# Row maxima of layer 1 started 32 product steps later with their loads placed behind the weight pieces, and the third row tile's input read into a second buffer

## The chip, the cores and the metric

The kernel runs on one core of one Trainium2 chip. A core has five instruction streams that run beside each other: TensorE (PE, with its weight loads shown as PEld), VectorE (DVE), ScalarE (ACT), GpSimd (POOL) and SyncE (SP). SP does no arithmetic; it issues most of the DMA transfers, one after the other, and a transfer whose buffer is not free yet holds up those behind it. ACT and POOL issue some transfers as well. The metric is the time of one execution on the device in microseconds; a kernel's time is the median of its runs.

## What is computed

Two layers over 2048 latent tokens of width 1024 and 256 context tokens. The change lies in layer 1, which is 2-D neighbourhood attention with 16 heads of width 64:

```python
h = rms_norm(x, norm_g[i]) * (1 + scale) + shift
q, k, v, z = jnp.split(jnp.dot(h, w_in), 4, axis=-1)
...
s_lat = jnp.einsum('bqhd,brkhd->bhqrk', qr, kb) * scale + bias
s_lat = jnp.where(col_mask, s_lat, -jnp.inf)
s_ctx = jnp.einsum('bqhd,bchd->bhqc', qr, k_ctx) * scale
p = jax.nn.softmax(jnp.concatenate([s_lat, s_ctx], axis=-1), axis=-1)
...
y = jnp.dot(o * jax.nn.silu(z_x), w_out)
```

The token grid has 32 rows of 64 columns; each query sees a window of 8 x 16 latent keys and all context keys. The softmax subtracts the maximum of each query's row of scores. The kernel computes these maxima ahead of the attention, in a pass of their own.

## The kernel before

The 2304 tokens (context first) are 18 row tiles of 128, numbered 0 to 17; tiles 0 and 1 are context. Float32 operands are split into a high and a low part, and a product takes three matmuls for each of the 8 pieces of the inner dimension (`mm3_steps`, L131 to L133). One such triple is a product step; a cell (t, j), row tile t by 512 columns j, has 8 steps.

Every instruction is issued by one engine in a fixed order. That order is not the program's text alone: when the kernel is built, a scheduler with its own estimates of durations orders each engine's instructions, taking among those that it holds to be ready the one that stands first in the text. `issue_after(x)` binds it: what is traced inside the block comes behind x on x's engine. On the chip the order stays as it is, whether the estimates were right or not.

Three stages follow each other around the change.

**`odd_qk`, the query/key stage.** Cells run over the row tiles with j = 2, 3 (keys), 0, 1 (queries) and 4 (first half of the values). Each tile's input is made ready by `prep`: `transposed` (L338) loads 128 x 1024 values of x1 into a buffer x (L346, on SP), ScalarE squares them into a PSUM bank, POOL makes the reciprocal root, VectorE scales, TensorE transposes; `modulate` scales and shifts on ScalarE, VectorE writes the parts hhi and hlo (two buffers each), and ScalarE's queue stores the result to H (L382) for the next stage. The buffer x exists once, so the next tile's load waits for that store. Tiles 0 and 1 are prepared at the end of the stage before, tile 2 after the cells of tile 0, and so on. Behind a cell of products, ScalarE squares its result (osq), VectorE sums it (oss), POOL takes the root (L218, L220), VectorE scales (onat, L1545), TensorE transposes (L1554) and ScalarE evicts (oqh). The pool osA, on the left side of the memory, is opened here; its buffer hx, of the size of x, is used for the last row tile alone.

**`odd_vz`, the value/gate stage.** It starts with tiles 15, 16 and 17 and then goes down to 0; j = 5 (second half of the values), 6 and 7 (gates, with VectorE's product L1639, transposes L1642 and ScalarE's ozt), and 4 for tiles 0 to 14. The 65 cells are 520 product steps; the first cells are (15,5), (16,5), (15,6), (16,6), (15,7), (16,7). The weights of a column block are 8 pieces of 256 KB (`od_steps`, `split_steps`): each is loaded into one of three buffers wraw (L422, on SP; `self.wload` is the last such load that was traced) and split by ScalarE (w3h for j = 7) and VectorE (w3l, L426), both bound behind the eviction of the cell in which the piece is traced. `turn(3)` traces three pieces a cell; the last three of j = 7 are traced in the stage's third cell.

Woven into the products are the row maxima, `maxes`: for each of 16 heads the keys mk (L1670, one load for two heads) and a bias table mtab (L1672) are loaded, POOL adds the row and the column mask to the table (L1673, L1674), and 16 steps follow. Every fourth step loads a strip of queries mq (L1682), which ScalarE writes into mz; each step has a matmul against the context keys (L1688), one against a rectangle of latent keys (L1695), and VectorE reduces both to maxima (L1690, and L1701 with the table). They share five PSUM banks mx. `row` transposes a head's maxima and stores them to M1.

`weave(main, side, ratio, lag, head)` traces both: after each step of main it adds ratio to due, which starts at -head x ratio, and traces one step of side for each whole unit. It binds each step of main behind the side step lag + 1 back. Here the ratio is 0.57 and the lag 15; the 256 side steps are the maxima.

**`odd_attention`.** Its loads go through `load` (L113), which binds each behind the one before, so SP issues them as one chain: the query parts of head 1, first keys, values, the two bias tables, context keys, the query parts of head 0, further keys, the context values V1c and the mask maskk. The memory of this stage lies over that of odd_vz; POOL then adds the mask to the tables (L1782). The first scores are against the context (kc, L1785 and L1786); scores against the latent keys (kt) get their bias on VectorE (L1944), which needs the masked tables.

Of the kernel before, what the change touches and what calls it, by code (L numbers as in the profile page):

```python
# [10 lines left out]
F32 = mybir.dt.float32  # L11
F32R = mybir.dt.float32r
# [5 lines left out]
P = 128  # L18
D = 1024
# [3 lines left out]
T = SEQ + CTX  # L23
# [38 lines left out]
def rect(kind, g, c):  # L62

    (r, nr), (k, nk) = reach(kind, 0, g), reach(kind, 1, c)
    while nr * nk < 256:
        k, nk = (k, nk + 1) if k == 0 else (k - 1, nk + 1)
    return (r, nr), (k, nk)


def even(a, n):  # L70

    b = a // 2 * 2
    return b, (a + n + 1) // 2 * 2 - b, a - b


def pieces(kind, ax, g, a, n):

    blocks, u = BLOCKS[kind][ax], AXES[ax][2]
    out = []
    for p in range(n):  # L80
        i = blocks.index((g, a + p) if (g, a + p) in blocks else (1, a + p - u * (g - 1)))
        if out and out[-1][1] + out[-1][2] == i:
            out[-1][2] += 1
        else:
            out.append([p, i, 1])
    return out


class Kern:
# [240 lines left out]
        self.prp = self.pool(es, name, bufs=2, side=side, reuse_waits="tile")  # L330
        self.hbufs, self.wbufs = bufs, wbufs

    def prep(self, l, t, src, pp, tag, last=None):

        parts = None if l else self.parts()
        return self.modulate(l, t, *self.transposed(t, src, pp, tag, None, parts), last)

    def parts(self):  # L338
        return [self.tl(self.prp, [P, KD, P], "h" + z, F32R, bufs=self.hbufs) for z in ("hi", "lo")]
# [1 line left out]
    def transposed(self, t, src, pp, tag, xp, parts):  # L341

        nc, sp = self.nc, self.prp
        pool, tg = xp or (sp, "x")
        x = self.tl(pool, [P, D], tg, bufs=1 if tg == "x" else None)
        self.xload = nc.sync.dma_start(x[:], src[t * P : t * P + P, :])  # L346
        ss = self.tl(sp, [P, 2], "ssx")
        ps = [self.tl(pp, [P, 4, P], tag[0], bufs=tag[1]) for _ in range(2)]
        if parts:
            self.act(parts[1][:].rearrange("p k t -> p (k t)"), x[:], AF.Square, accum_out=ss[:, 0:1])  # L350
            self.rpow(ss[:, 1:2], ss[:, 0:1], 1.0 / D, EPS)
            nc.vector.tensor_scalar(out=x[:], in0=x[:], scalar1=ss[:, 1:2], scalar2=None, op0=ALU.mult)
        else:
            for g in range(2):
                self.act(ps[g][:].rearrange("p k t -> p (k t)"), x[:, self.HALF[g]], AF.Square, accum_out=ss[:, g : g + 1])
            nc.gpsimd.tensor_scalar(out=ss[:, 1:2], in0=ss[:, 0:1], scalar1=ss[:, 1:2], scalar2=EPS * D, op0=ALU.add, op1=ALU.add)
            nc.gpsimd.tensor_tensor(out=ss[:, 1:2], in0=ss[:, 1:2], in1=self.mhalf[:, :1], op=ALU.pow)
            nc.vector.tensor_scalar(out=x[:], in0=x[:], scalar1=ss[:, 1:2], scalar2=D ** 0.5, op0=ALU.mult, op1=ALU.mult)
        for k in range(KD):
            nc.tensor.transpose(ps[k // 4][:, k % 4, :], x[:, k * P : k * P + P], self.ident[:])  # L360
        return x, ps, parts
# [1142 lines left out]
    def odd_qk(self, ws, win, hT):  # L1504
        nc = self.nc
# [5 lines left out]
        with ExitStack() as es:  # L1511
            sp = self.pool(es, "osA", bufs=2, side="left", reuse_waits="tile")
            pp = self.pool(es, "opA", bufs=2, space=PSUM, reuse_waits="tile")
# [2 lines left out]
            nc.vector.tensor_scalar(out=qkg[:, 0:1], in0=qkg[:, 0:1], scalar1=0.125, scalar2=None, op0=ALU.mult)  # L1516
            self.later += [self.od_steps(win, j, ws, lambda: self.done) for j in (0, 1)]
            pend, kt = [], {}
            prep = lambda t, last=None: self.prep(1, t, self.x1, pp, ("px", 2), last)

            def cell(t, j):
                if (t, j) == (NT - 3, 3):
# [90 lines left out]
    def odd_vz(self, ws, win, hT):  # L1613
        nc = self.nc
        self.z1 = self.scr("z1", (KD, P, SEQ), F32)
        self.M1 = self.scr("M1", (16, SEQ), F32)
        NR, NC = (len(b) for b in BLOCKS["q"])
        with ExitStack() as es:
            sp = self.pool(es, "osB", bufs=2, side="left", reuse_waits="tile")
            mp = self.pool(es, "omB", bufs=2, side="left", reuse_waits="tile")  # L1620
            pp = self.pool(es, "opB", bufs=2, space=PSUM, reuse_waits="tile")
            mk = self.tl(mp, [P, NR + NC], "maskq", bufs=1)
# [33 lines left out]
            def row(h, mc):  # L1656
                pt = self.tl(pp, [P, 512], "mx", bufs=5)
                nc.tensor.transpose(pt[:16, :P], mc[:], self.ident[:])
                r = self.tl(mp, [P, P], "mr", F32R, bufs=1)
                self.act(r[:16], pt[:16, :P], AF.Copy, scale=-1.0)  # L1660
                for g in range(4):
                    nc.gpsimd.dma_start(self.M1[h, g * 512 : g * 512 + 512].rearrange("(a c b) -> c a b", a=8, c=4),
                                        r[4 * g : 4 * g + 4].rearrange("c (a b) -> c a b", a=8).bitcast(F32))

            def maxes():
                for h in range(16):
                    j, b = h // 2, (h % 2) * 64
                    if b == 0:
                        k = self.tl(mp, [P, T], "mk", F32R, bufs=2)
                        nc.sync.dma_start(k[:].bitcast(F32), self.K1[j])  # L1670
                    tb = self.tl(mp, [P, NR, NC], "mtab", bufs=2)
                    nc.sync.dma_start(tb[:], self.i["rpb_q"][h].rearrange("p (r c) -> p r c", r=NR))  # L1672
                    nc.gpsimd.tensor_tensor(out=tb[:], in0=tb[:], in1=mk[:, :NR].unsqueeze(2).to_broadcast([P, NR, NC]), op=ALU.add)  # L1673
                    nc.gpsimd.tensor_tensor(out=tb[:], in0=tb[:], in1=mk[:, NR:].unsqueeze(1).to_broadcast([P, NR, NC]), op=ALU.add)  # L1674
                    m = self.tl(mp, [P, 16, 5], "mm")
                    nc.vector.memset(m[:], -3e38)
                    kl = k[:, CTX:].rearrange("d (r c) -> d r c", r=32)
                    for R in range(16):
                        g, c = divmod(R, 4)
                        if c == 0:  # L1680
                            q = self.tl(mp, [P, 512], "mq", F32R, bufs=1)
                            nc.sync.dma_start(q[b : b + 64].bitcast(F32), self.Q1[0, j, b : b + 64, g * 512 : g * 512 + 512])  # L1682
                            zt = zq[h % 2][g % 2]
                            self.by_tile(zt[b : b + 64], q[b : b + 64])
                        lh = zt[:, c * P : c * P + P]
                        if c % 2 == 0:
                            pc = self.tl(pp, [P, 2, CTX], "mx", bufs=5)
                        nc.tensor.matmul(pc[:, c % 2, :], lh, k[:, :CTX], start=True, stop=True)  # L1688
                        if c % 2 == 1:
                            nc.vector.tensor_reduce(out=m[:, R - 1 : R + 1, 0], in_=pc[:], axis=AX.X, op=ALU.max)  # L1690
                        (r0, nr), (c0, w) = rect("q", g, c)
                        ps = self.tl(pp, [P, 512], "mx", bufs=5)
                        a, n, d = even(c0, w)
                        ps = ps[:, : nr * n].rearrange("p (r c) -> p r c", r=nr)
                        mm = nc.tensor.matmul(ps, lh, kl[:, r0 : r0 + nr, a : a + n], start=True, stop=True)  # L1695
                        ps = ps[:, :, d : d + w]
                        n = 1
                        for ro, ri, rn in pieces("q", 0, g, r0, nr):
                            for co, ci, cn in pieces("q", 1, c, c0, w):
                                s = ps[:, ro : ro + rn, co : co + cn]  # L1700
                                nc.vector.tensor_tensor_reduce(out=s, in0=s, in1=tb[:, ri : ri + rn, ci : ci + cn], scale=1.0,  # L1701
                                                               scalar=-3e38, op0=ALU.add, op1=ALU.max, accum_out=m[:, R, n : n + 1])
                                n += 1
                        yield mm
                        if R == 5 and h:
                            row(*turn)
                    mc = self.tl(mp, [P, 16], "mc", bufs=1)
                    nc.vector.tensor_reduce(out=mc[:], in_=m[:], axis=AX.X, op=ALU.max)
                    turn = (h, mc)
                row(*turn)  # L1710

            first = [NT - 3, NT - 2, NT - 1]
            cells = self.cells(first + list(range(NT - 3))[::-1], (4, 5, 6, 7), lambda t, j: (j > 4 or t < NT - 3) and (j < 6 or t >= NCT))
            gemms = self.stream(cells, hT, cell, lambda t: self.reload(1, t))
            self.weave(gemms, maxes(), 0.57, 15)


    def odd_attention(self, out, right, left, wout):
# [508 lines left out]
```

## Time and profile before

| | us |
|---|---|
| runs | 3557.17 median (3553.28 to 3560.04, 3 runs) |
| profiled execution | 3555.91 |
| its span, first to last instruction | 3554.1 |
| TensorE busy | 3451.6 |
| VectorE, ScalarE, POOL busy | 2438.8, 1452.0, 1239.9 |
| mean granted TensorE clock | 0.987 |

Terms and durations are from the profiled execution. An instruction group is given by line, engine, operation and the names of the program (out<-in); a number in square brackets is the time in which the engine stood idle before it, with the instruction or transfer that ended the wait. Matmuls overlap, so the start to start time is below the duration shown. A table of stretches gives from and to, the length, busy time and count of instructions on PE, PEld, DVE, ACT and POOL, the clock granted to TensorE (1.00 is full), the share of the DMA engines and the GB/s. Where a table is asked for the instructions of one line, it has PE and PEld alone.

### The profile page before, as it was taken

To read this page: it belongs to the slowest core of one execution; us is meant where nothing else is said; L and a number is where in the kernel's file an instruction comes from. 1 tells how busy PE (TensorE), PEld (TensorE's weight loads), DVE (VectorE), ACT (ScalarE), POOL (GpSimd) and SP (SyncE) were. 2 spreads that over 40 slices of the span, in tenths; PEclk is the share of its full clock that TensorE was granted. 3 is DMA by queue.
4 is the path that set the end of the run, shared out by engine and by line. 5 is a ranking of instruction groups with operands and counts; after the bars stand their busy time and mean duration, and the time that the engine had idled before them with its cause. 6 is when DMAs were issued, how large, how long until landed. Compare 5 with 4: busy or idle time off the path is not lost. (4 is left out here: it accounts for less than half of the span.)

```text
span 3554.1 us, 54063 instructions
## 1 busy us (share of the span) xinstructions
PE 3451.6 (97%) x19460; PEld 2666.4 (75%) x19460; DVE 2438.8 (69%) x4798; ACT 1452.0 (41%) x2647; POOL 1239.9 (35%) x1400
## 2 busy tenths in 40 slices
PE   7999999999999999999999999999899999999999
PEld 6888987888896666655556878888688887656577
DVE  4677656888885777768876655445587874666875
ACT  5445542111113544546664345445322222555532
POOL 1333431111111333422211134334334442888852
PEclk9999999999999999999999999999999999999999
DMA  7555555232325142334535664455745447888684
GB/s 256 143 158 158 148 141 150 95 109 92 92 76 168 59 136 80 103 107 133 173 91 140 127 185 147 137 156 146 234 157 165 154 157 188 216 219 219 193 243 78
DMA packets 379596, 526.75 MB, mean 148 GB/s; under 512 B 34633, under 2 KB 254233, under 8 KB 372882
## 3 DMA queue, kind: packets, MB, share of 16 engines
q1 hardware_dynamic: 326450, 405.32, 39.6%
q0 software_dynamic: 29856, 82.14, 9.2%
q10 hardware_dynamic: 23024, 35.85, 2.9%
q8 instruction: 154, 2.52, 0.3%
q14 instruction: 112, 0.92, 0.1%
HBM read 344.39 MB, written 196.60 MB: 152 GB/s over the span
## 5 line engine op out<-in xcount | busy, mean ns | idle before, releaser
L699 DVE TENSOR_REDUCE mm<-mx 128x1 f32<-128x512 f32 (+1 forms) x656 | 388.7, 630 | 81.8 <-PE mx L698 74.8
L108 ACT ACTIVATE apt<-st 128x1024 f32<-128x1024 f32 (+1 forms) x296 | 300.2, 1015 | 312.2 <-PE st L1168 297.4
L1175 DVE TENSOR_TENSOR acc<-acc,apt 128x1024 f32<-128x1024 f32 x256 | 340.8, 1331 | 80.7 <-ACT apt L108 61.4
L1168 PE MATMUL st<-aq,akh 64*128 64x512 f32 x1728 | 313.3, 410 | 1.1 <-ACT apt L108 0.8
L1078 PE MATMUL av<-apt,av 128*64 128x512 f32 x1152 | 267.2, 601 | 0.0
L1944 DVE TENSOR_TENSOR opt<-st,tab 128x64 f32<-128x64 f32 (+10 forms) x576 | 144.5, 318 | 146.6 <-PE st L1786 72.3
L698 PE MATMUL mx<-mk,mq 96*128 96x512 f32 (+1 forms) x656 | 235.8, 373 | 0.9 <-DMA mq<-QC 0.7
L1825 POOL TENSOR_TENSOR oacc<-oacc,opt 128x576 f32<-128x576 f32 (+5 forms) x192 | 222.4, 1183 | 39.1 <-DVE oacc L1809 15.1
L1168 PE MATMUL st<-aq,akl 64*128 64x512 f32 (+1 forms) x1152 | 231.2, 392 | 0.0
L108 ACT ACTIVATE u<-gm 128x352 f32<-128x352 f32 (+1 forms) x140 | 68.5, 497 | 370.2 <-PE gm L133 208.1
L1168 PEld LDWEIGHTS st<-aq,akh 64*128 64x128 f32 x1728 | 153.6, 186 | 83.4 <-ACT apt L108 28.7
L1701 DVE CUSTOM_DVE_ANT_1 mx<-mx,mtab 128x225 f32<-128x225 f32 (+10 forms) x576 | 183.8, 338 | 38.9 <-PE mx L1695 30.7
L1078 PEld LDWEIGHTS av<-apt,av 128*64 128x64 f32 x1152 | 76.6, 137 | 136.3 <-issue 135.3
L108 ACT ACTIVATE opt<-opt 128x930 f32<-128x930 f32 (+8 forms) x130 | 104.3, 805 | 108.9 <-DVE opt L1944 101.9
L698 PEld LDWEIGHTS mx<-mk,mq 96*128 96x128 f32 x656 | 121.2, 188 | 13.1 <-issue 1.1
L1168 PEld LDWEIGHTS st<-aq,akl 64*128 64x128 f32 (+1 forms) x1152 | 112.4, 185 | 23.5
L220 POOL TENSOR_TENSOR oss<-oss,mhalf 128x8 f32<-128x8 f32 x68 | 113.3, 1667 | 5.0
L131 PE MATMUL gm<-w1h,hhi 128*128 128x512 f32 x280 | 113.0, 404 | 0.0
L1785 PE MATMUL st<-q,kt 128*128 128x480 f32 (+5 forms) x256 | 98.9, 388 | 14.1 <-DVE opt L1944 10.1
L133 PE MATMUL gm<-w1h,hlo 128*128 128x512 f32 x280 | 110.6, 395 | 0.0
L132 PE MATMUL gm<-w1l,hhi 128*128 128x512 f32 x280 | 110.3, 394 | 0.0
L1690 DVE TENSOR_REDUCE mm<-mx 128x2 f32<-128x512 f32 x128 | 88.1, 689 | 32.2 <-PE mx L1688 30.7
(686 smaller groups left out, 9748.6 us busy)
## 6 DMA issues: line engine op xcount, KB each, us to landing
q<-Q SPq DMA_DIRECT2D x48, 512.0 KB
H<-x ACTq DMA_DIRECT2D x33, 512.0 KB
adaw<-ada_w SPq DMA_DIRECT2D x64, 256.0 KB
wraw<-w_od SPq DMA_DIRECT2D x64, 256.0 KB
K1t<-okt POOLq DMA_DIRECT2D x32, 512.0 KB, 9.6
kt<-K1t SPq DMA_DIRECT2D x32, 512.0 KB
x<-H SPq DMA_DIRECT2D x31, 512.0 KB
mtab<-rpb_q SPq DMA_DIRECT2D x16, 899.0 KB
```

The lines of the kernel that those rows point to most:

```text
L108: return self.nc.scalar.activation(out, in_, func, **kw)
L131: self.nc.tensor.matmul(out, lh(k), rh(k), start=start and j == 0, stop=False)
L133: yield self.nc.tensor.matmul(out, ll(k), rh(k), start=False, stop=stop and j == n - 1)
L220: return g.tensor_tensor(out=out, in0=out, in1=self.mhalf[:, : shp[1]], op=ALU.pow)
L698: mm = nc.tensor.matmul(ps[:, :w], q[:A_QK, (t % 6) * P : (t % 6) * P + P], k[:A_QK, k0 : k0 + w], start=True, stop=True)
L699: nc.vector.tensor_reduce(out=m[:, t, n : n + 1], in_=ps[:, :w], axis=AX.X, op=ALU.max)
L1078: mm = nc.tensor.matmul(O[j, nb][i * 64 : i * 64 + 64, :w], V[j, kt // TT][:, kt % TT, i * 64 : i * 64 + 64], pts[:, i, :w], start=n == 0, ...
L1168: mm = nc.tensor.matmul(ps[:, o // 64, :w], k[o : o + r, kb, kq], Q[o : o + r, qb, :w], start=m == 0, stop=m == 4)
L1175: added = nc.vector.tensor_tensor(out=acc[:, :, :w], in0=a[:, :, :w], in1=pts[:, :, :w], op=ALU.add)
L1701: nc.vector.tensor_tensor_reduce(out=s, in0=s, in1=tb[:, ri : ri + rn, ci : ci + cn], scale=1.0, scalar=-3e38, op0=ALU.add, op1=ALU.max, a ...
L1825: self.psum = nc.gpsimd.tensor_tensor(out=a, in0=a, in1=pts[:, :, a0 - r0 : a1 - r0, :], op=ALU.add)
L1944: bias = nc.vector.tensor_tensor(out=pt[:, d[0], d[1]], in0=ps[:, d[0], d[1]], in1=tabs[j][i][:, ri : ri + rn, ci : ci + cn], op=ALU.add)
```

## The change

The input of tile 2 in layer 1 is read into hx of pool osA instead of x. The loads of mk and mtab are bound behind the last weight load that was traced, on SP. The maxima start with a head of 32: the first is traced after 34 product steps, in the stage's fifth cell, where it was 2; the 256th after 482, where it was 450. At that point all weight pieces have been traced. The loads of mq are not bound.

```diff
--- before.py
+++ after.py
@@ -330,10 +330,10 @@
         self.prp = self.pool(es, name, bufs=2, side=side, reuse_waits="tile")
         self.hbufs, self.wbufs = bufs, wbufs
 
-    def prep(self, l, t, src, pp, tag, last=None):
+    def prep(self, l, t, src, pp, tag, last=None, xp=None):
 
         parts = None if l else self.parts()
-        return self.modulate(l, t, *self.transposed(t, src, pp, tag, None, parts), last)
+        return self.modulate(l, t, *self.transposed(t, src, pp, tag, xp, parts), last)
 
     def parts(self):
         return [self.tl(self.prp, [P, KD, P], "h" + z, F32R, bufs=self.hbufs) for z in ("hi", "lo")]
@@ -342,7 +342,7 @@
 
         nc, sp = self.nc, self.prp
         pool, tg = xp or (sp, "x")
-        x = self.tl(pool, [P, D], tg, bufs=1 if tg == "x" else None)
+        x = self.tl(pool, [P, D], tg, bufs=1 if tg != "pr" else None)
         self.xload = nc.sync.dma_start(x[:], src[t * P : t * P + P, :])
         ss = self.tl(sp, [P, 2], "ssx")
         ps = [self.tl(pp, [P, 4, P], tag[0], bufs=tag[1]) for _ in range(2)]
@@ -1516,7 +1516,7 @@
             nc.vector.tensor_scalar(out=qkg[:, 0:1], in0=qkg[:, 0:1], scalar1=0.125, scalar2=None, op0=ALU.mult)
             self.later += [self.od_steps(win, j, ws, lambda: self.done) for j in (0, 1)]
             pend, kt = [], {}
-            prep = lambda t, last=None: self.prep(1, t, self.x1, pp, ("px", 2), last)
+            prep = lambda t, last=None: self.prep(1, t, self.x1, pp, ("px", 2), last, (sp, "hx") if t == 2 else None)
 
             def cell(t, j):
                 if (t, j) == (NT - 3, 3):
@@ -1665,11 +1665,12 @@
             def maxes():
                 for h in range(16):
                     j, b = h // 2, (h % 2) * 64
-                    if b == 0:
-                        k = self.tl(mp, [P, T], "mk", F32R, bufs=2)
-                        nc.sync.dma_start(k[:].bitcast(F32), self.K1[j])
-                    tb = self.tl(mp, [P, NR, NC], "mtab", bufs=2)
-                    nc.sync.dma_start(tb[:], self.i["rpb_q"][h].rearrange("p (r c) -> p r c", r=NR))
+                    with self.tc.issue_after(self.wload.ins):
+                        if b == 0:
+                            k = self.tl(mp, [P, T], "mk", F32R, bufs=2)
+                            nc.sync.dma_start(k[:].bitcast(F32), self.K1[j])
+                        tb = self.tl(mp, [P, NR, NC], "mtab", bufs=2)
+                        nc.sync.dma_start(tb[:], self.i["rpb_q"][h].rearrange("p (r c) -> p r c", r=NR))
                     nc.gpsimd.tensor_tensor(out=tb[:], in0=tb[:], in1=mk[:, :NR].unsqueeze(2).to_broadcast([P, NR, NC]), op=ALU.add)
                     nc.gpsimd.tensor_tensor(out=tb[:], in0=tb[:], in1=mk[:, NR:].unsqueeze(1).to_broadcast([P, NR, NC]), op=ALU.add)
                     m = self.tl(mp, [P, 16, 5], "mm")
@@ -1712,7 +1713,7 @@
             first = [NT - 3, NT - 2, NT - 1]
             cells = self.cells(first + list(range(NT - 3))[::-1], (4, 5, 6, 7), lambda t, j: (j > 4 or t < NT - 3) and (j < 6 or t >= NCT))
             gemms = self.stream(cells, hT, cell, lambda t: self.reload(1, t))
-            self.weave(gemms, maxes(), 0.57, 15)
+            self.weave(gemms, maxes(), 0.57, 15, 32)
 
 
     def odd_attention(self, out, right, left, wout):
```

## The prediction

> **What bounds the kernel now.** I read the page first, then busy time by stretches along the span, then the order of TensorE's instructions where a stretch was not full, and last what each queue waited for there.
>
> ```profile
> span 3554.1 us, 54063 instructions
> PE 3451.6 (97%) x19460; PEld 2666.4 (75%) x19460; DVE 2438.8 (69%) x4798; ACT 1452.0 (41%) x2647; POOL 1239.9 (35%) x1400
> ```
>
> TensorE sets the time; 3554.1 - 3451.6 = 102.5 us of the span are not busy, and only time that it loses (idle, or at a lower clock) can be won. Three stretches (times from the span's start) lie near the change:
>
> ```profile
> 2100.00:2140.00 40.00, 35.14 (x163) 28.51 (x162) 23.47 (x40) 19.09 (x39) 21.86 (x29) 0.96 0.73 236
> 2540.00:2580.00 40.00, 27.09 (x105) 21.75 (x104) 23.27 (x54) 11.26 (x18) 14.72 (x6) 0.79 0.59 204
> 2600.00:2640.00 40.00, 40.00 (x200) 33.60 (x200) 31.50 (x119) 11.53 (x19) 20.74 (x16) 1.00 0.44 143
> ```
>
> The columns are PE, PEld, DVE, ACT, POOL busy (instructions), granted clock, DMA share, GB/s. A full stretch holds 200 matmuls in 40 us, 0.2 us each. The first two lie at the start of the query/key stage and at the start of the value/gate stage. They hold 163 and 105: (200 - 163) x 0.2 = 7.4 us lost in the first (4.9 us of it idle), (200 - 105) x 0.2 = 19 us in the second (12.9 us idle, the rest the granted clock of 0.79). These are the most that the change can win. TensorE's own waits:
>
> ```profile
> 2117.62 0.87 PE L1554 MATMUL tp<-ident,onat 128*128 128x128 f32 x4 [3.62 <-DVE onat L1545]
> ...
> 2550.68 0.58 PE L1688 MATMUL mx<-mk,mz 128*128 128x256 f32 x1 [6.46 <-ACT mz L108]
> ...
> 2564.82 0.66 PE L132 MATMUL gm<-w3l,hhi 128*128 128x512 f32 x1 [3.86 <-DVE w3l L426]
> ...
> 2570.21 1.12 PE L1642 MATMUL tp<-ident,ovz 128*128 128x128 f32 x4 [2.59 <-DVE ovz L1639]
> ```
>
> **Part one: tile 2's input in a buffer of its own.** No instruction is added. What moves is the order of loads into the single buffer x.
>
> ```profile
> SPq L346 <- DMA H<-x: 14.5, 1, 14.5
> ```
> ```profile
> 2107.23 0.52 SPq L346 DMA_DIRECT2D x<-x  x1
> ```
> ```profile
> 2114.18 0.60 ACT L108 ACTIVATE px<-x 128x512 f32<-128x512 f32 x1 [4.12 <-DMA x<-x]
> ```
> ```profile
> 2116.12 0.75 DVE L1562 SCALAR_TENSOR_TENSOR oql<-tp,oqkg,oqh 128x512 fp32r<-128x512 f32 x1 [7.55 <-ACT oqh L108]
> ```
>
> SP stands 14.5 us at tile 2's load until tile 1's store H<-x has left x, and tile 3's load goes out only at 2107.23, after tile 2's own store. ScalarE reaches tile 3's squares, waits 4.12 us for that load, and its eviction oqh stands behind them; VectorE waits 7.55 us for oqh, its product onat (L1545) follows, and TensorE's transposes wait 3.62 us for onat. With tile 2 in hx, tile 3's load needs only tile 1's store (done by about 2087.5, where SP is released), so it can be issued some 20 us sooner, and the 4.12 us go. The next tile in x is then 4, whose load moves up with tile 3's store. Queued behind tile 2's load on SP are the gain vector and eight weight pieces; they can only gain. Bounds: 7.4 us at best. At worst hx is late itself: its memory belongs to the pool opened at this stage, over tiles of the stage before, and no row shows when they leave it. The last could be an output buffer:
>
> ```profile
> 2085.76 0.86 POOL L1310 DMA_DIRECT2D x<-py  x1 [4.60 <-DVE py L1308]
> ```
> ```profile
> x<-py POOLq DMA_DIRECT2D x36, 256.0 KB, 4.1
> ```
>
> That DMA has landed by 2085.76 + 0.86 + 4.1 = 2090.7, some 3 us after x came free: a loss of 3 us. I take a gain of **5.5 us**, nearer the gain since the wait named by the row goes for certain.
>
> **Part two: the row maxima 32 steps later, behind the weights.** The loads, matmuls, mask adds and reductions of the maxima stay the same in number. Two loads a head (24 of 88 loads with the mq ones) get an order on SP; it binds only for the first heads, since later weight loads are long gone. The beginning before:
>
> ```profile
> 2538.15 0.33 SPq L1670 DMA_DIRECT2D mk<-K  x1
> 2538.58 1.78 SPq L1672 DMA_DIRECT2D mtab<-rpb_q  x1
> 2540.41 1.40 SPq L1682 DMA_DIRECT2D mq<-Q  x1
> 2541.86 0.58 SPq L1672 DMA_DIRECT2D mtab<-rpb_q  x1
> 2542.48 0.47 SPq L1670 DMA_DIRECT2D mk<-K  x1
> 2543.06 1.59 SPq L422 DMA_DIRECT2D wraw<-w_od  x3
> ```
> ```profile
> 2550.00 0.63 ACT L108 ACTIVATE mz<-mq 64x512 fp32r<-64x512 f32 x1 [7.34 <-DMA mq<-Q]
> ```
> ```profile
> 2549.48 3.20 POOL L1673 TENSOR_TENSOR mtab<-mtab,maskq 128x1798 f32<-128x1798 f32 x1 [11.27 <-DMA mtab<-rpb_q]
> ...
> 2556.89 7.32 POOL L1674 TENSOR_TENSOR mtab<-mtab,maskq 128x1798 f32<-128x1798 f32 x2
> ```
> ```profile
> 2556.36 9.61 DVE L426 TENSOR_TENSOR w3l<-wraw,w3h 128x512 fp32r<-128x512 f32 x3 [1.90 <-ACT w3h L108]
> ```
> ```profile
> 2540.00:2556.00 16.00, 9.54 (x37) 7.75 (x36) 3.40 (x6) 3.93 (x6) 6.51 (x4) 0.79 0.99 343
> ```
>
> Two mk and two mtab (4.1 MB) go ahead of the last weight pieces; the DMA engines are full (0.99, 343 GB/s). So mq comes late (6.46 us on TensorE), the pieces of w3 come late and their subtractions stretch to 9.61 us beside the mask adds (3.86 us), and the gate product stands behind them on VectorE (2.59 us). Afterwards the six pieces of 256 KB go first. They share three buffers, and a buffer is free when its piece is split, which the code ties to the end of a cell: the last three pieces can go out when the three before are split, some time after step 16 of the stage (2527 + 16 x 0.71 = 2538.4; 0.71 us a step is worked out below). With two turns of some 4 us each (estimate: 0.8 MB at 343 GB/s is 2.3 us, and the split) that is 2546.5. w3 is then split by about 2551, and its first cell starts at step 32 (2549.7) with the early pieces: the 3.86 us go. mk is issued at 2546.5 and lands near 2553 (0.5 + 1.2 MB at 343 GB/s is 5 us, and some latency), about where TensorE may take its first row maximum (step 34, 2551). The first mtab lands near 2557 and needs its two adds, 3.2 + 3.7 us: VectorE cannot begin before 2564. If the fixed order of VectorE expects it sooner, the gate products and then TensorE wait behind it, as in the 2.59 us row. I leave 7.5 us of such waits with their slow clock: a gain of **11.5 us**, between 4 (one wait goes, the other two stay) and 19 (all go).
>
> **What the later maxima bring at the end.** This term has the other sign. weave ties product step N to row-maximum step 0.57 N - 16, so a maximum may stand 27 product steps behind its place, no more.
>
> ```profile
> 2527.00:2551.00 24.00, 9.66 (x25) 4.50 (x24) 0.94 0.92 301
> ...
> 2965.70:2997.70 32.00, 17.35 (x45) 8.27 (x44) 1.00 0.98 254
> ```
> ```profile
> 2965.58 0.30 PE L1695 MATMUL mx<-mk,mz 128*128 128x288 f32 x1
> ...
> 2997.82 0.96 PE L1785 MATMUL st<-q,kc 128*128 128x512 f32 x3 [0.69 <-ACT ovz L108]
> ```
>
> The windows count L133, one per product step. The first maximum (place: step 2) runs after step 25, the last (place: step 449) with 45 of 520 steps to go, at step 475: 26 late, at the limit. With the head of 32 the limit lies at step 507: 12 to 13 steps of 32.0 / 45 = 0.71 us, 8.9 us, stay behind the last maximum instead of 32.2 us. It does start less late now, so whether the lag grows back is the question; layer 0's stage shows it, which starts with a head of 20 and a ratio of 1.06 (maxima L698, then product steps L133):
>
> ```profile
> 617.00:640.00 23.00, 8.67 (x24) 4.34 (x24) 1.00 0.32 105
> ...
> 660.00:1081.00 421.00, 197.90 (x552) 102.11 (x552) 1.00 0.29 90
> ```
> ```profile
> 617.00:640.00 23.00, 11.14 (x33) 6.02 (x32) 1.00 0.32 105
> ...
> 660.00:1081.00 421.00, 184.76 (x527) 98.91 (x527) 1.00 0.29 90
> ```
>
> There 24 maxima go with 33 steps at first, far under 1.06, and only the limit brings them to 552 in 527. So I expect the limit here too. Behind the last maximum stands the attention stage's chain of loads on SP:
>
> ```profile
> SPq L113 <- PE mx L1695: 14.8, 1, 14.8
> SPq L113 <- DMA V1c<-ovz: 10.8, 2, 7.3
> ```
> ```profile
> 2997.16 0.35 SPq L113 DMA_DIRECT2D maskk<-maskk  x1
> ```
> ```profile
> 3004.99 4.70 POOL L1782 TENSOR_TENSOR tab<-tab,maskk 128x1034 f32<-128x1034 f32 x2 [0.62 <-DMA maskk<-maskk]
> ```
> ```profile
> 3007.38 1.17 DVE L1944 TENSOR_TENSOR opt<-st,tab 128x32 f32<-128x32 f32 x6 [30.40 <-POOL tab L1782]
> ```
> ```profile
> 2968.00:3004.00 36.00, 34.86 (x155) 26.96 (x153) 2.51 (x3) 11.31 (x19) 8.35 (x13) 1.00 1.03 273
> ```
>
> SP waits 14.8 us for the last maximum, then issues two queries, keys, values, tables and, last, maskk: 7.9 MB by the code's shapes. From the last maximum to the first biased score it takes 3007.38 - 2965.58 = 41.8 us, 9.6 us beyond the first score at 2997.82; waits of SP for stores of the same stage (V1c) are in it, which a later chain mostly meets no more. At 273 GB/s the 7.9 MB take 29 us; with 2 us of latency (estimate: the end of the DMA row less bytes over rate) and 2.4 us of mask add (half of 4.70) that is 33 us, 24.5 us beyond the stage's end: 15 us more than now. At the 343 GB/s of the window above it is 23 + 4.4, 9 us more; if nothing is squeezed, the whole shift, 32.2 - 8.9 = 23 us; if the lag does not grow back, nothing. TensorE has only 16 context scores to do meanwhile, and these need the second query. I take a loss of **14 us**, near the row of the same place.
>
> By the Trainium skill, page "DMA: Bandwidth & Descriptors", section "Specifications", HBM gives one core up to about 358 GB/s: 7.9 MB in 22 us, 8 us of loss, a sum of -9; this trace stays under it here (273).
>
> **The sum.** -5.5 - 11.5 + 14 = -3 us on the profiled execution (3555.91 us, its span 3554.1), so 3552.9; the median of the runs, 3557.17, is 1.3 above it, so I say **3554 us**.
>
> **The rivals.** *The chain is not late* (0.18): the maxima do not fall back by more than some 10 steps, the last ends 20 us or more before the stage's end, and the waits for V1c set the chain as before. For it: VectorE is busy 31.5 of 40 us, not full. Against: so it was in the stage before, at the limit from end to end. -17 + 2 = -15: 3542. *The chain is late in full* (0.17, the slower side): the loads keep their 41.8 us, since rings and stores are shared, and the start wins 8 and 4: 23 - 12 = +11: 3568. It decides once the chain takes over 36 us. *The change does not do what it says at the start* (0.15): the first maximum, its order fixed ahead, still comes too soon for mk and mtab, now the only loads in front of it; the wait of 6.5 us and the slow clock move to 2553 and only some 5 us are won there, 4 at tile 3: 14 - 9 = +5 to +8: 3562 to 3565.
>
> **How the numbers follow.** The forecast has 0.50, with its own range 3547 to 3561. 0.2% (7 us) is about what can be told from no change. Faster by more: 0.18 and 0.12 of the forecast, 0.30. Slower by more: 0.14 of the late chain, 0.10 of the last rival, 0.02 of the forecast, 0.26. The rest, 0.44, is within. The range of 3542 to 3567 leaves out about 0.09 below and 0.09 above.
>
> **What would show it.** Right: no wait of ScalarE at tile 3's squares; all w_od pieces before the first mk on SP; no wait on w3l; 12 to 13 product steps after the last maximum; SP's wait for mx ending within 10 us of the first score; and TensorE idle over 10 us between the last product and the first biased score. Wrong: 30 or more steps after the last maximum, a first score that does not wait, or waits of over 10 us at the first maxima.

## The result

| | us |
|---|---|
| before, median of 9 runs | 3555.33 (3548.76 to 3560.89) |
| the change, median of 9 runs | 3564.05 (3559.90 to 3570.66) |
| ratio | 1.0025, 95% interval 1.0014 to 1.0037 |
| profiled execution of the change (before: 3555.91) | 3565.63 |

The kernel became slower, by 9 us, where -3 was forecast. The time lies inside the range given (3542 to 3567), near its upper end.

The head of the page and four stretches of the span, with the columns of the tables shown before:

```profile
span 3563.9 us, 54063 instructions
PE 3453.2 (97%) x19460; PEld 2666.8 (75%) x19460; DVE 2431.0 (68%) x4798; ACT 1449.8 (41%) x2647; POOL 1243.9 (35%) x1400
```
```profile
2100.00:2140.00 40.00, 36.49 (x175) 29.25 (x174) 24.89 (x43) 24.01 (x52) 26.04 (x32) 1.00 0.76 235
2540.00:2580.00 40.00, 34.83 (x154) 28.20 (x153) 17.32 (x53) 14.15 (x23) 15.85 (x8) 0.91 0.73 247
2980.00:3000.00 20.00, 5.22 (x24) 3.86 (x22) 0.00 (x0) 1.10 (x3) 4.50 (x8) 0.71 1.07 267
3000.00:3020.00 20.00, 14.06 (x36) 9.71 (x38) 4.36 (x17) 6.57 (x11) 7.20 (x4) 0.50 1.04 260
```

TensorE's busy time is the same within 2 us, and the span is 9.8 us longer: the time went into idle. The two stretches that the change aimed at are fuller (175 and 154 matmuls, were 163 and 105). The loss is in the last two: 60 matmuls in 40 us, at full DMA engines, and the clock falls to 0.50 in the idle time.

Four events cut the span into parts that can be compared. They are the last store of layer 0 (POOL, x<-py), the first product of the value/gate stage (gm<-w1h,hhi), its last product, and the first biased score on VectorE. Each part runs from start to start of their rows; the rest goes from there to the end of the span. The rows of the change:

```profile
2083.88 0.85 POOL L1310 DMA_DIRECT2D x<-py  x1 [4.59 <-DVE py L1308]
```
```profile
2525.63 0.50 PE L131 MATMUL gm<-w1h,hhi 128*128 128x512 f32 x1
...
2984.83 0.39 PE L133 MATMUL gm<-w1h,hlo 128*128 128x512 f32 x1
```
```profile
3014.46 1.16 DVE L1945 TENSOR_TENSOR opt<-st,tab 128x32 f32<-128x32 f32 x6 [36.02 <-POOL tab L1783]
```

The same four of before are 2085.76, 2527.09, 2996.74 and 3007.38. All twelve kernels, in us (the other ten are the experiments below):

| kernel | query/key | value/gate | last product to first biased score | rest |
|---|---|---|---|---|
| before | 441.33 | 469.65 | 10.64 | 546.7 |
| the change | 441.75 | 459.20 | 29.63 | 549.4 |
| hx_only | 445.82 | 470.66 | 10.59 | 548.5 |
| late_only | 444.39 | 457.11 | 30.11 | 550.0 |
| lag33 | 443.90 | 466.84 | 29.13 | 550.0 |
| ratio612 | 446.97 | 457.06 | 13.38 | 549.9 |
| hx_first | 437.43 | 469.26 | 11.10 | 549.2 |
| hx_alt | 442.22 | 467.63 | 11.11 | 545.0 |
| chain_order | 442.35 | 458.61 | 20.66 | 562.5 |
| head_only | 445.18 | 465.17 | 30.14 | 551.6 |
| both612 | 436.70 | 457.71 | 11.03 | 548.3 |
| both66 | 438.45 | 462.44 | 8.00 | 548.4 |

One profile of a stage is good to some 4 us: before, late_only, lag33 and head_only have the same query/key stage, and show 441.3 to 445.2. From before to the change the parts give +0.4, -10.5, +19.0 and +2.7, and the stretch ahead of them -1.9, which no edit explains: +9.7, the difference of the profiled executions.

**At tile 3** SP's order is the point. The loads of the change at the start of the stage, and what ScalarE waits for:

```profile
2084.99 0.33 SPq L346 DMA_DIRECT2D x<-x  x1
2085.41 0.42 SPq L1515 DMA_DIRECT2D oqkg<-od_gain  x1
2085.93 0.45 SPq L346 DMA_DIRECT2D hx<-x  x1
```
```profile
2090.98 0.60 ACT L108 ACTIVATE px<-hx 128x512 f32<-128x512 f32 x1 [12.04 <-DMA hx<-x]
...
2125.83 0.60 ACT L108 ACTIVATE px<-x 128x512 f32<-128x512 f32 x1 [3.61 <-DMA x<-x]
```

The load of tile 3 into x, which has to wait for tile 1's store, stands ahead of tile 2's into hx. So hx, free or not, goes out at 2085.93, where tile 2's load into x went out at 2087.42 before; counted from the last store of layer 0 that is 2.1 us, where it was 1.7. ScalarE's wait at tile 3 is gone; one of 3.61 us has appeared at tile 4. TensorE's wait for onat, 3.62 us before, is 1.60 now:

```profile
2121.97 0.63 PE L1554 MATMUL tp<-ident,onat 128*128 128x128 f32 x4 [1.60 <-DVE onat L1545]
```

But over the whole stage TensorE stands idle for 5.9 us, where before it was 4.9.

**At the first maxima** all weight pieces go ahead of mk, and no wait for w3l is left:

```profile
2546.51 1.71 SPq L422 DMA_DIRECT2D wraw<-w_od  x2
2548.39 0.33 SPq L1671 DMA_DIRECT2D mk<-K  x1
2548.81 0.86 SPq L1673 DMA_DIRECT2D mtab<-rpb_q  x2
```
```profile
2549.92 0.63 PE L1642 MATMUL tp<-ident,ovz 128*128 128x128 f32 x4 [1.38 <-DVE ovz L1639]
2556.28 0.58 PE L1689 MATMUL mx<-mk,mz 128*128 128x256 f32 x1 [3.42 <-DMA mk<-K]
```

Of 6.46, 3.86 and 2.59 us of waits, 3.42 and 1.38 remain.

**At the end** the last maximum, the count of L133 behind it (the two numbers in brackets are products on PE and weight loads on PEld), the first score and the whole chain's stretch:

```profile
2976.54 0.30 PE L1696 MATMUL mx<-mk,mz 128*128 128x288 f32 x1
```
```profile
2976.84:2985.30 8.46, 4.75 (x12) 2.25 (x12) 1.00 0.83 188
```
```profile
3004.77 1.62 PE L1786 MATMUL st<-q,kc 128*128 128x512 f32 x3 [19.55 <-DMA q<-Q]
```
```profile
2976.87:3011.90 35.03, 15.22 (x52) 0.67 1.02 257
```
```profile
3012.04 4.73 POOL L1783 TENSOR_TENSOR tab<-tab,maskk 128x1034 f32<-128x1034 f32 x2 [24.34 <-PE st L1787]
```

Twelve product steps are left behind the last maximum, as forecast. The chain starts at 2976.87; TensorE has nothing to do until the second query lands at 3004.77, and VectorE has no biased score to work on until the first of the two mask adds is done (the last row: two adds in 4.73 us). In these 35 us the DMA engines are full (1.02) and move 257 GB/s x 35.03 us = 9.0 MB, of which the chain up to maskk is 7.9.

### The profile page after: what moved, and what is told of

It is laid out like the page before. It is cut to its first block, busy times and chain, and to the rows that moved or that the text cites. A ratio compares the mean times of both kernels' runs of the same rounds, so it can differ in the third digit from the quotient of the medians.

```text
span 3563.9 us, 54063 instructions
## 1 busy us (share of the span) xinstructions
PE 3453.2 (97%) x19460; PEld 2666.8 (75%) x19460; DVE 2431.0 (68%) x4798; ACT 1449.8 (41%) x2647; POOL 1243.9 (35%) x1400
## 5 line engine op out<-in xcount | busy, mean ns | idle before, releaser
L1702 DVE CUSTOM_DVE_ANT_1 mx<-mx,mtab 128x217 f32<-128x217 f32 (+12 forms) x576 | 183.6, 339 | 53.3 <-PE mx L1696 40.6
L133 PE MATMUL gm<-w1h,hlo 128*128 128x512 f32 x280 | 110.3, 394 | 0.0
## 6 DMA issues: line engine op xcount, KB each, us to landing
K1t<-okt POOLq DMA_DIRECT2D x32, 512.0 KB, 10.1
```

Source lines behind the costliest of these rows:

```text
L133: yield self.nc.tensor.matmul(out, ll(k), rh(k), start=False, stop=stop and j == n - 1)
```

## The experiments

Three questions: what did the spare buffer win, what did the later start of the maxima win, and what makes the end slow? Ratios are to runs of before on the same chip.

**hx_only: the spare buffer alone**, with the first three pieces of the change's diff (in `prep` and `transposed`) as they are, and

```diff
-            prep = lambda t, last=None: self.prep(1, t, self.x1, pp, ("px", 2), last)
+            prep = lambda t, last=None: self.prep(1, t, self.x1, pp, ("px", 2), last, (sp, "hx") if t == 2 else None)
```

> Tile 2's input in hx alone; the row maxima start and load as before. Theory now: the order on SP puts tile 3's load (into x, waiting for tile 1's store) ahead of tile 2's load into hx, so tile 2 comes no sooner and the wait moves to tile 4: 0 us against before (within 3), the time from the stage's opening at 2085 us to the first value/gate product as before within 1 us. Rival, the prediction's term: 5.5 us faster.

3553.76 us against 3556.46, ratio 0.9993 (0.9984 to 1.0003): nothing that can be told from no change. The query/key stage took 445.82 us, no less than in the four kernels without the buffer; that is 4.5 us above before, where the expectation had the same within 1 us.

**late_only: the change without the spare buffer.**

```diff
-            prep = lambda t, last=None: self.prep(1, t, self.x1, pp, ("px", 2), last, (sp, "hx") if t == 2 else None)
+            prep = lambda t, last=None: self.prep(1, t, self.x1, pp, ("px", 2), last)
```

> The change without hx: tile 2 read into x as before. Theory now: like the changed kernel, 8 to 10 us slower than before, made of 10 us won at the first maxima and 19 us lost before the first biased score of the attention. Rival (hx did win its 5.5 us in the changed kernel): 14 us slower than before.

3568.76 us, ratio 1.0033 (1.0021 to 1.0045), +12: between the two expectations. With the change itself at 1.0025 this bounds the spare buffer's worth to a few us either way; it doesn't settle it.

**lag33: before, with only the end moved.**

```diff
-            self.weave(gemms, maxes(), 0.57, 15)
+            self.weave(gemms, maxes(), 0.57, 33)
```

> Only the end: head 0 and no order on SP as before, but a lag of 33 in place of 15, so that the limit of the last maximum moves from product step 475 to 507, as with the head of 32. Theory: nothing won at the start, the load chain of the attention starts with 13 product steps left, its first biased score comes some 19 us later against the last product: 17 to 20 us slower than before. Rival: the loss in the changed kernel has another source (other loads, the order of POOL); then within 5 us of before.

3575.74 us, ratio 1.0047 (1.0034 to 1.0059): 19 us slower by the medians, 17 by the ratio. The first score and the first biased score:

```profile
3014.27 1.62 PE L1785 MATMUL st<-q,kc 128*128 128x512 f32 x3 [19.01 <-DMA q<-Q]
```
```profile
3024.00 1.17 DVE L1944 TENSOR_TENSOR opt<-st,tab 128x32 f32<-128x32 f32 x6 [36.19 <-PE st L1786]
```

The start of the stage is that of before here, and the gap at the end is that of the change, 29.13 us against 10.64. The end's loss needs nothing else of the change.

**ratio612: the change, with more maxima per product step,** so that they catch up: 45 steps stay behind the last one instead of 12.

```diff
-            self.weave(gemms, maxes(), 0.57, 15, 32)
+            self.weave(gemms, maxes(), 0.612, 15, 32)
```

> The whole change with a ratio of 0.612 in place of 0.57: the maxima still start behind the weights, but the last one lies 45 product steps before the stage's end, as before. Theory: the start's 10 us are kept and the end's 19 us are gone: 8 to 11 us faster than before. Rival: VectorE, busy 31.5 of 40 us, becomes the bound when the maxima are packed 7% closer, TensorE waits for reductions all through the stage: no faster than before.

3547.25 us, ratio 0.9968 (0.9958 to 0.9978), 9 us faster than before by the medians, 11 by the ratio. The value/gate stage stays as short as in the change (457.06 us, there 459.20), and the gap falls from 29.63 to 13.38. With lag33 this settles the end from both sides: the time of the last maximum decides, and the late start, with its order on SP, wins some 10 us once the end is given back.

**head_only: before, with the head of 32 and no order on SP.**

```diff
-            self.weave(gemms, maxes(), 0.57, 15)
+            self.weave(gemms, maxes(), 0.57, 15, 32)
```

> The head of 32 steps alone: no order on SP, no spare buffer. Theory (the start is won by the weights going first, which the order on SP does): the first row maximum's loads still stand ahead of the last weight pieces, the gate product's wait stays, and the start wins 4 to 6 us of the 10.5; with 18 to 20 lost at the end the time is 3567 to 3572. Rival (the later place of the row maxima alone puts their loads behind the weights): the start wins all 10, as in the change: 3562 to 3566.

3570.27 us, ratio 1.0047 (1.0035 to 1.0059). SP and TensorE of this kernel:

```profile
2538.78 0.83 SPq L1672 DMA_DIRECT2D mtab<-rpb_q  x1
2539.65 0.63 SPq L1670 DMA_DIRECT2D mk<-K  x1
2540.39 1.68 SPq L422 DMA_DIRECT2D wraw<-w_od  x3
```
```profile
2561.66 0.79 PE L132 MATMUL gm<-w3l,hhi 128*128 128x512 f32 x1 [7.46 <-DVE w3l L426]
```

The maxima start later by TensorE's order, but their loads are still issued ahead of the last three weight pieces, and the wait on w3l grows to 7.46 us. The stage takes 465.17 us: 4.5 won of 10.5, about what one profile can tell. TensorE in the first 80 us of the stage (busy, matmuls, clock, DMA share, GB/s) of before, lag33, head_only and the change:

```profile
2527.09:2607.09 80.00, 67.09 (x298) 0.89 0.62 202
```
```profile
2528.03:2608.03 80.00, 68.91 (x310) 0.94 0.62 200
```
```profile
2525.11:2605.11 80.00, 70.00 (x315) 0.91 0.63 207
```
```profile
2525.63:2605.63 80.00, 74.83 (x343) 0.96 0.68 220
```

The change has 45 matmuls more than before, head_only 17; but lag33, whose first maximum stands where it stood before, has 12 more too, and a stage 2.8 us shorter. So most of what the start wins comes with the order on SP.

**chain_order: the change, with the attention stage's chain in another order.**

```diff
             Q[0, 1] = query(0, 1)
-            kt.append(chunk(0, 0))
-            V[0] = values(0)
-            tabs[0] = tables(0)
             kc[0] = keys(0, 0, CTX, kcp, "kc")
             Q[0, 0] = query(0, 0)
-            kt.append(chunk(0, 1))
-            values_ctx(0, V[0])
+            tabs[0] = tables(0)
             mk = self.tl(ap, [P, NR, NC], "maskk", bufs=1)
             self.load(mk[:], self.i["maskk"].rearrange("p (r c) -> p r c", r=NR))
+            kt.append(chunk(0, 0))
+            V[0] = values(0)
+            values_ctx(0, V[0])
+            kt.append(chunk(0, 1))
```

> The whole change, and in the attention stage's chain of loads the first query's keys, the second query, the tables and the mask go ahead of the value tiles and the local keys. Theory (the end loses 19 us because 6.4 MB stand ahead of the second query and 7.8 MB ahead of the mask, at some 230 GB/s): only 3.5 MB stand ahead of the first context score, so it starts 15 to 16 us after the chain's first load instead of 27.9, and the first biased score comes about 27 us after it instead of 37.6; 8 to 10 us of the 19 come back, 3555 us, ratio to before 0.999 to 1.001. Rival (the chain is a run of issue costs and latencies, whatever its order): the first biased score stays 36 to 38 us behind the chain's start and the time stays at 3562 to 3566.

3561.68 us, ratio 1.0019 (1.0008 to 1.0030). Three rows of TensorE, one of VectorE, and two stretches with PE alone (busy, instructions, clock, DMA share, GB/s):

```profile
2989.60 1.62 PE L1786 MATMUL st<-q,kc 128*128 128x512 f32 x3 [9.53 <-DMA q<-Q]
...
3034.78 0.56 PE L1786 MATMUL st<-q,kt 128*128 128x264 f32 x1 [4.31 <-DMA kt<-K1t]
3036.47 0.59 PE L1787 MATMUL st<-q,kt 65*128 65x264 f32 x1 [1.14 <-DMA kt<-K1t]
```
```profile
3000.34 1.17 DVE L1945 TENSOR_TENSOR opt<-st,tab 128x32 f32<-128x32 f32 x6 [27.04 <-PE st L1787]
```
```profile
3020.34:3030.34 10.00, 9.74 (x69) 1.00 1.08 234
3030.34:3040.34 10.00, 4.55 (x27) 0.71 0.82 195
```

The order does decide when each piece lands, by its bytes: the chain starts at 2971.72, so the first score comes 17.9 us after it (27.9 in the change), the first biased score 28.6 us (37.6). In that the theory holds and the rival falls. But of 9 us hardly anything stays. The DMA engines are still full until 3030 (1.08), and TensorE now waits for a later key tile and falls to a clock of 0.71. Counted in matmuls behind the last product, the lead over the change is 9.5 us at the 100th, 1.8 at the 300th and none at the 1000th. (The rest grows by 13 us in all; the other 4 us come after the 1500th, and no run here explains them.) So the time came out about where the rival had it, for another reason, and the ratio's interval overlaps that of the change. This order of loads only chose who waits for the bytes; other orders were not tried.

**hx_first: hx_only, with tile 3's load bound behind tile 2's on SP.**

```diff
-        self.xload = nc.sync.dma_start(x[:], src[t * P : t * P + P, :])
+        with self.tc.issue_after(self.hxload.ins) if (tg, t) == ("x", 3) and self.hxload else ExitStack():
+            self.xload = nc.sync.dma_start(x[:], src[t * P : t * P + P, :])
+        self.hxload = self.xload if tg == "hx" else None
```

> Part one alone, with SP told to issue tile 2's load into the spare buffer ahead of tile 3's load. Theory (part one won nothing because SP stands at tile 3's load, 2085 us, before it reaches the spare buffer): tile 2's load goes out some us earlier than in part one alone, where it was issued 0.9 us behind tile 3's; the 12 to 13 us that ScalarE waits for it shrink, TensorE's 1.7 us at tile 2's transposes go, tile 4's wait stays: the query/key stage 1 to 2 us shorter than with part one alone, too little to tell from it in the time (ratio to before 0.998 to 1.000). Rival (the order on SP was the only thing wrong): all 5.5 us come, ratio 0.9985 or less, and no ScalarE wait at tile 4.

3549.58 us, ratio 0.9987 (0.9976 to 0.9998), 5 us faster. SP and ScalarE:

```profile
2078.08 0.33 SPq L348 DMA_DIRECT2D hx<-x  x1
2082.39 0.33 SPq L348 DMA_DIRECT2D x<-x  x1
```
```profile
2083.44 0.60 ACT L108 ACTIVATE px<-hx 128x512 f32<-128x512 f32 x1 [6.58 <-DMA hx<-x]
...
2121.49 0.60 ACT L108 ACTIVATE px<-x 128x512 f32<-128x512 f32 x1 [4.25 <-DMA x<-x]
```

Against hx_only, tile 2 goes out 6.8 us earlier (2084.90 there) and tile 3, whose wait for the store sets its time, 1.6 (2084.00). With the binding the scheduler also moved the load of the gain vector oqkg ahead, to 2072.38 from 2084.42; no run separates the two moves. Tile 4's wait stays, as the theory said, but costs TensorE little. TensorE's busy time and matmuls in the first 60 us from the last store of layer 0, in hx_first, hx_only and before:

```profile
2081.80:2141.80 60.00, 57.70 (x278) 1.00 0.63 190
```
```profile
2082.08:2142.08 60.00, 54.19 (x250) 0.97 0.61 181
```
```profile
2085.76:2145.76 60.00, 55.14 (x261) 0.97 0.58 180
```

The change, with the order of hx_only, has 268 matmuls in such a stretch. The three kernels with tile 2 first and no other tile moved (this one, both612 and both66) take 437.4, 436.7 and 438.5 us for the stage. The four with the change's order take 441.8 to 447.0, the four without the buffer 441.3 to 445.2. TensorE's idle time in the stage, its length less the busy time, says the same: 2.3, 1.7 and 3.5 us in the three, 5.9 to 8.1 in the four with the change's order, 4.9 to 7.7 in the four without the buffer. The whole time alone could not tell: the interval of hx_only's ratio overlaps this one. On the amount the rival was right by the stage (its ratio, 0.9985 or less, was just missed), on tile 4's wait the theory.

**hx_alt: all even tiles from 2 on in hx, the loads in order of the tiles.**

```diff
+        with self.tc.issue_after(self.xlast.ins) if not parts and t > 2 and self.xlast else ExitStack():
             self.xload = nc.sync.dma_start(x[:], src[t * P : t * P + P, :])
+        self.xlast = self.xload
...
-(sp, "hx") if t == 2 else None
+(sp, "hx") if t > 1 and t % 2 == 0 else None
```

> Part one carried on: all even tiles from 2 on use the spare buffer, the odd ones the first, loads issued in the order of the tiles. Theory (what is scarce is the turnaround of a single buffer, load, squares, modulation, store, some 20 us a tile, so one tile moved only moves the wait to tile 4): tile 4's load goes out before 2110 instead of at 2122, ScalarE's 3.6 us at its squares go, and the query/key stage is 3 to 5 us shorter; ratio to before 0.9985 to 0.9995. Rival (the waits on onat have another cause and the input tiles are never short): the stage stays at its 441 to 447 us and TensorE's waits for onat keep their sum of 6 to 8 us; ratio 1.000 within 0.001.

3551.20 us, ratio 0.9989 (0.9978 to 1.0000). Tile 4 is loaded at 2099.21 and its squares no longer wait, but at 442.22 us the stage is longer than hx_first's, no shorter than without the buffer. Another wait stands there:

```profile
2106.28 0.63 ACT L108 ACTIVATE w2h<-wraw 128x512 fp32r<-128x512 f32 x1 [4.17 <-DMA wraw<-w_od]
```

ScalarE has to split a weight piece first, the eviction oqh behind it comes late, and TensorE waits 1.12 us for onat; after the next pieces, for which ScalarE waits too, it is 2.53. These waits for onat sum to 4.8 us, before to 4.9. So the theory falls at its stage: with the tiles there in time, by these rows, the weight pieces come last. The ratio is nonetheless that of hx_first; this profile has a short rest (545.0), which no edit explains, and that stays open.

**both612 and both66: the change with both repairs,** tile 2's load first and the ratio at 0.612, or at 0.66, where 77 product steps stay behind the last maximum.

> The whole change with both repairs: the ratio raised to 0.612, and tile 2's load ahead of tile 3's on SP. Theory (the order on SP cost the 4 to 5 us of part one, the lag at the end cost 16 to 19, and the two places don't touch): the gains add, 3539 to 3543 us, ratio to before 0.9945 to 0.9965, and the first product of the value/gate stage comes 437 to 439 us after the last store of layer 0, against 441 to 447 without the order. Rival (the gain with tile 2 first was a short stage by chance): ratio 0.997, as with the raised ratio alone.

> The same with ratio 0.66: 77 product steps stay behind the last row maximum instead of 45. Theory (at 45 steps the chain of loads is hidden but for the waits on V1c and the mask, which an earlier last maximum doesn't move, and more maxima per product step cost TensorE nothing where it is full): within 3 us of the 0.612 version. Rival (the last biased scores still wait for the chain): first biased score 7 to 10 us after the last product instead of 13, and 3 to 6 us faster.

both612: 3538.51 us against 3555.76, ratio 0.9960 (0.9946 to 0.9973), 17 us faster than before by the medians, 14 by the ratio, the lowest median of the twelve. By the stages the gains add: the query/key stage takes 436.70 us (446.97 in ratio612), the value/gate stage 457.71, the gap 11.03. By the time alone the rival's 0.997 is not out, since it lies inside the interval. The first biased score:

```profile
2985.00 1.16 DVE L1948 TENSOR_TENSOR opt<-st,tab 128x32 f32<-128x32 f32 x6 [30.78 <-POOL tab L1786]
```

both66: 3542.64 us, ratio 0.9965 (0.9953 to 0.9978): no further gain. The gap falls to 8.00 us, as the rival said, from 11.03, but the value/gate stage is 4.7 us longer, little more than one profile can tell; that the denser weave takes what the end gives back is not shown. What is shown is that the last maximum no longer sets the chain's start here: it runs at 2922.29, and the chain starts at 2934.18, behind a load (x<-H) for which SP waits 22.2 us.

## Why the prediction was wrong

**Part one, -5.5: measured 0.** The step that failed is that "tile 3's load needs only tile 1's store" and "can be issued some 20 us sooner, and the 4.12 us go", taken as the whole story. It was issued 22 us sooner (2084.99, before 2107.23), and the 4.12 us went; but the fixed order of SP put it ahead of tile 2's load into hx, which therefore still waited for x, and a wait of 3.61 us came up at tile 4. TensorE's idle time in the stage went from 4.9 to 5.9 us. The prediction looked at what is "queued behind tile 2's load on SP", and not at what might come in front of it. Its bound for a loss was for another reason (the memory of hx still in use), and there is something in that too: in hx_first SP waits 5.2 us at the load into hx, by the profile for a product of the stage before, and hx comes free only 4.3 us before x does (2078.08 and 2082.39). With the order put right, hx_first, both612 and both66 show 437.5 on average against 443.7 of the four kernels without the buffer: -6.2, close to the 5.5. So the size was about right, of an edit that the change didn't make.

**Part two, -11.5: measured -10.5 in the stage.** Weights first, no wait on w3l and part of the two other waits left: as worked out. By matmuls it is a little less, 45 more in the first 80 us at 0.2 us each, 9.0 us. Head_only, with the head alone, keeps the wait on w3l and gets 17 of the 45, so the order on SP does its part. The rival "the change does not do what it says at the start" is thereby out.

**The end, +14: measured +19.0.** Mechanism and count of steps (12) are as forecast; that the lag grows back to its limit, read off layer 0, was right. The step that failed is the size of one term: "at 273 GB/s the 7.9 MB take 29 us", 31 with its 2 us of latency, where it took 35.2 (2976.87 to 3012.04). The rate was nearly right, 257 GB/s, but it is the rate of everything that moves, and the chain doesn't have the engines to itself: 9.0 MB moved in its 35 us, so that its own 7.9 MB went at 225 GB/s. By the queues of the packets 0.5 MB of it are stores (V1c), and nearly 0.6 MB stand on SP's queue beyond the chain: the next head's tables, issued at 3002.32, before maskk has landed. Before it was no different: 10.1 MB moved during its chain (2965.91 to 3004.99), 1.6 of them on other queues than SP's. The 2.4 us of mask add stood as said (3012.04 to 3014.46). From last maximum to first biased score it took 3014.46 - 2976.54 = 37.9 us, against 33 forecast and 41.8 before; the rival "the chain is late in full" kept the 41.8 and said that it decides from 36 on. That point was passed, and its +11 is near the +9.7 that came; its reason, rings and stores that are shared, holds in half: SP waits for no V1c store in this chain any more, but such stores are 0.5 of the 1.1 MB that moved beside it.

The limit of about 358 GB/s that the Trainium skill states in "DMA: Bandwidth & Descriptors", section "Specifications", is again not reached by the chain as a whole: 257 GB/s with the engines' share at 1.02. By it the loss would have been an estimated 8 us. For 2.7 us, while the tables landed (2993.87 to 2996.60), the measured rate was 385, above that limit.

**The signs.** No wait at tile 3's squares: seen, with a new one at tile 4. Weights before mk, no wait on w3l, 12 steps, idle over 10 us before the first biased score: seen. "SP's wait for mx ending within 10 us of the first score" was put badly: it ended 8 us before the last product, but the score itself then slid to 28 us after it.

The two errors, 5.5 and 5, had the same sign, and the sum was small against its terms. Either alone would have left some +3, which can't be told from no change; together they made the kernel slower.

## What to carry to other kernels

A buffer that lets one load go early gains only if that load is also early in its queue: read what stands ahead of it, and what the scheduler will move forward because of the new buffer. When work is pushed later, look at whom its end releases, here a chain of 7.9 MB of loads; what cured it here was to let it catch up (a higher rate in the weave); the one reordering that was tried of the loads that it holds back won nothing clear of noise. A chain of loads is costed with what the queue issues behind it, too, since that shares the engines before the chain has landed.

## What the runs showed of the hardware

With the DMA engines full the rate still depends on what moves. In the change's chain, by the times of its packets, the first query pieces (64 partitions, 8 KB packets) moved 1.6 MB in 6.8 us (228 GB/s, share 1.00), the values (512 B packets) 1 MB in 5.1 us beside 0.26 MB of a store (267 GB/s, share 1.17), and the tables (128 partitions, 4136 B packets) 1 MB in 2.7 us (385 GB/s, share 1.04). So the busy share alone doesn't tell the rate. Whether the size of the packets or the number of partitions decides isn't separated.

A load issued later on the same queue can move beside an earlier one. In the change, 384 packets of 4136 B run between 3008 and 3014: by their count 128 are maskk's and 256 the next head's two tables, of which the first was issued 2.5 us behind it. The mask add starts 12.2 us after maskk's issue (2999.81 to 3012.04), where before it was 7.8 (2997.16 to 3004.99). In the change's row the releaser named is a matmul that ended at the same time; head_only has the same wait with the transfer named:

```profile
3018.00 4.72 POOL L1782 TENSOR_TENSOR tab<-tab,maskk 128x1034 f32<-128x1034 f32 x2 [24.85 <-DMA maskk<-maskk]
```

TensorE's clock can stay down long after its idle time is over. In the change it is granted 0.50 from 2988.58 on, 3.8 us after the last product started; the context scores start at 3004.77, and TensorE is then busy for 14.1 of 15.2 us (to 3020) without a rise. It is back at 1.00 from 3022.72 on, 18 us after the work came back.
